# A streaming encoder layer on one core: another place for the last conv norms, and cross attention opened inside the last mixing tile

## The chip, the cores and the metric

One core of one Trainium2 chip runs the whole kernel in one launch. The metric is the device time of an execution in microseconds; the time of a kernel is the median of its runs.

## The reference

One layer of a chunk-causal hybrid encoder, in float32, for a prompt of 2048 frames and a sample group of 8 streams with 16 frames each (128 rows in all, which make a 17th tile beside the prompt's 16). D_MODEL is 1024.

```python
proj = h @ w_in                                   # h = rmsnorm(x, g_mix_pre)
q, k, v, u_val, u_gate = split(proj)              # 512 columns each
att = band_attention(q, k_ext, v_ext, ..., rel_bias)   # 8 heads x 64, own chunk of 64 + 8 previous
u = u_val * sigmoid(u_gate)
c = depthwise_conv(u_ext, conv_w) + conv_b        # causal, width 31, 512 channels
c = silu(layernorm(c, cln_g, cln_b))
y = concat([att, c]) @ w_out
x = x + rmsnorm(y, g_mix_post)
x = x + rmsnorm(memory_attention(rmsnorm(x, g_mem_pre), mk, mv, w_mq, w_mo), g_mem_post)
f = (silu(h @ w_gate) * (h @ w_up)) @ w_down      # h = rmsnorm(x, g_ffn_pre), hidden 2816
x = x + rmsnorm(f, g_ffn_post)
```

Memory attention has 4 heads of 256 and 256 memory tokens. For the prompt, its keys and values are made from `mem_prompt`; for the sample streams they are cached. The outputs are both groups' rows and the updated caches (attention K and V, conv rows, memory K and V).

## The kernel before

**Arithmetic.** Each float32 operand of a product is split into a high part (a rounded copy, made by a cast on ACT) and a low part (the difference, made by a subtraction on VectorE or on POOL). A product is three matmuls, high by high, high by low, low by high: `mm3` (L281 to L285, widths 128 to 384) and `mm3h` (L287 to L291, two halves of 512 columns, so six matmuls a block and 48 a tile).

**Stages.** `phase_mem` makes the memory's keys and values, and folds w_mq into the keys and w_mo into the values, so that cross attention has two weight blocks a row of blocks: f1 (scores) and f2 (values), eight blocks each. `phase_proj` makes q, k, v and the conv branch; `attention` runs the band attention; `mixout` applies w_out, tile by tile; `phase_cross`, `gate_up` and `down` follow.

**Projection.** Three groups of six tiles (the last has the sample tile in it), each in two sub-groups x = 0 and 1 of 384 and, in the last group, 256 prompt or sample columns. In a group come the GLU columns, then v, then K and Q by blocks j = 0 to 3. The depthwise convolution is a list of generators, `vq` for VectorE (L517 to L524) and `pq` for ACT and POOL (L526 to L533), pumped between the products at a rate per group and at low priority. `conv_norm` (L535 to L558) is the layer norm of one tile: four transposes to PSUM (L538), statistics on VectorE (L540, L542), the reciprocal root (L294 to L301), the normalised rows (L546), four transposes back (L550), scale and bias on ACT (L553), tanh (L556), the product (L557) and the store to the DRAM tensor `cs` (L558). Its result `z` has two buffers. Before the change the norms of the last group's first five tiles are put on `vq` in pairs behind the convolutions, ahead of the v products (`pairs(tiles[:-1], cts)`), and the sample tile's norm comes last. The scheduler of the framework then lists each engine's instructions; an engine runs its list in order.

**Q, K and the head load.** Each Q/K product is cast (L691, L697), its low part taken (L692, L698), and stored to DRAM (`qs`, `ks`, L717). `head_load` brings a head's q and k (L780, 64 rows of 2048) and v (L781) back; head 0's load is issued inside the last group. Tags of odd and even heads are apart, so two heads fit at a time.

**Attention.** 128 units of one head and one prompt tile: scores (L856), softmax on VectorE (L793) with the exponential on ACT (L795), transposes (L873), values (L886). Sample steps are mixed in (`sample`, L798 on); their bias rows `bs` are eight small DMAs (L899), and their scores L816.

**Mixing.** 17 tiles, sample first (L979 on). `prep` loads a tile's `cs` and splits it; then 48 products and the post norm (L1053 squares on ACT, L1057 on VectorE, L1058 on POOL, store of x1). Beside it the sample rows' cross attention runs as a filler (`cross_sample`, L1065 on), with L1086 as the load of its weight blocks (w_mq, cached keys and values, w_mo) and `postnorm` (L335 to L340, the residual on POOL at L340) at its end.

**Cross attention.** `phase_cross` opened after the last mixing tile: the gains (L362), norm(0) (x1 load L1218, `rms` L304 to L309, L315, transposes L318, high part L319 on ACT, low part L320 on VectorE), then all eight f1 blocks (load L1209 to one of three staging buffers `stg`, cast L1212 on ACT, subtraction L1213, on POOL for blocks 1, 3 and 5), norm(1), scores(0), and so on: scores (L1224 on), `probs` (L1242 on, transposes L1245, L1248, L1249), `values` (L1252 on). f2 blocks were loaded by `more`, behind the last exponential of scores(0) and the split of the first probabilities. `issue_after(x)` makes what is issued inside it stand behind x on its engine.

## Time and profile before

| | |
|---|---|
| runs | 2968.06, 2971.57, 2972.08 us; median 2971.57 |
| profiled execution | 2970.86 us, span 2969.1 us, mean granted clock 0.989 |
| TensorE, VectorE, ACT, POOL busy | 2877.8, 2076.6, 1308.7, 1367.9 us |
| DMA | 500.04 MB in 198474 packets, mean 168 GB/s |
| idle of TensorE, 600 to 680 us | 24.0 us |
| idle of TensorE, 1140 to 1180 us | 11.35 us |

A line of a timeline reads: start (us), duration, engine, source line, operation, output<-input, shape, count, and in brackets how long the engine had been idle and what ended that. The names of tiles are those of the memory pools (`psb` PSUM; `sbf`, `sbr`, `sbx`, `flexb` SBUF; `qs`, `ks`, `vs`, `cs`, `f1s` DRAM).

### The profile page before, as it was taken

What the parts mean: (1) busy time and instruction counts of PE and PEld (TensorE: products, weight loads), DVE (VectorE), ACT (ScalarE), POOL (GpSimd) and SP (SyncE); (2) the same over time, 40 slices, a digit from 0 to 9 for tenths busy, and PEclk for the clock granted to TensorE, in tenths of its full rate; (3) what the DMA queues carried; (4) which work ended last, traced back from release to release, by engine and by line L of the source; (5) the groups of instructions that cost most, each with busy time, mean ns of one, the idle gap of its engine ahead of it and who ended that gap; (6) DMA issues with size and microseconds to landing.
All of it is one profiled execution on the core that took longest, in us unless ns stands there. A gap on an engine that the chain in (4) does not pass through costs nothing.

```text
span 2969.1 us, 45382 instructions
## 1 busy us (share of the span) xinstructions
PE 2877.8 (97%) x16740; PEld 2628.1 (89%) x16740; DVE 2076.6 (70%) x3024; ACT 1308.7 (44%) x2661; POOL 1367.9 (46%) x1247
## 2 busy tenths in 40 slices
PE   8999999979989998999999999999999999999998
PEld 8999999968978776888879999999999999888786
DVE  6697795958985334445459888787888998546655
ACT  4535354648973223333334333433344444433433
POOL 0268395720022223145447656365656775424413
PEclk9999999989999999999999999999999999999999
DMA  8635255557845664223355333644434446756654
GB/s 307 245 114 179 91 167 161 169 154 188 214 144 175 229 219 164 76 96 126 112 172 196 138 114 133 200 155 152 145 121 160 148 143 211 242 172 221 226 193 165
DMA packets 198474, 500.04 MB, mean 168 GB/s; under 512 B 18981, under 2 KB 87085, under 8 KB 189923
## 3 DMA queue, kind: packets, MB, share of 16 engines
q1 hardware_dynamic: 187931, 461.09, 48.2%
q0 software_dynamic: 10320, 36.05, 3.1%
q8 instruction: 131, 2.15, 0.3%
q14 instruction: 92, 0.75, 0.1%
HBM read 365.97 MB, written 141.81 MB: 171 GB/s over the span
## 4 chain that ended last, share of the span: by engine, by line
PE 42%; DMA 3%; POOL 2%; DVE 2%; issue 1%; ACT 0%; DVEq 0%; SPq 0%; POOLq 0%; ACTq 0%
PE psb L285 13%; PE psb L284 13%; PE psb L283 13%; PE psb L291 1%; DMA sbf<-in_w_down_dram 1%; DMA sbf<-x 1%; POOL sbf L1500 1%; PE psb L1355 1%; DMA sbf<-hn 1%; POOL sbf L340 0%; DVE sbr L1378 0%; DMA hn<-sbf 0%; DVE flexb L1440 0%; DVE sbr L1561 0%; DVE sbx L1378 0%
## 5 line engine op out<-in xcount | busy, mean ns | idle before, releaser
L283 PE MATMUL psb<-sbr 128*128 128x384 f32 (+3 forms) x2808 | 942.1, 337 | 3.3 <-ACT sbr L319 1.1
L284 PE MATMUL psb<-sbr 128*128 128x384 f32 (+3 forms) x2356 | 805.6, 342 | 2.4 <-DVE sbr L320 2.4
L285 PE MATMUL psb<-sbr 128*128 128x512 f32 (+3 forms) x1848 | 632.7, 344 | 2.2 <-DVE sbr L1561 2.2
L283 PEld LDWEIGHTS psb<-sbr 128*128 128x128 f32 x2808 | 530.5, 189 | 32.5 <-ACT sbr L1357 1.7
L285 PE MATMUL psb<-sbr,sbx 128*128 128x384 f32 (+2 forms) x1484 | 476.8, 322 | 0.0
L284 PEld LDWEIGHTS psb<-sbr 128*128 128x128 f32 x2356 | 445.0, 189 | 29.4 <-DVE sbr L320 2.7
L285 PEld LDWEIGHTS psb<-sbr 128*128 128x128 f32 x1848 | 348.0, 189 | 30.6 <-DVE sbr L1561 4.2
L291 PE MATMUL psb<-sbr 128*128 128x512 f32 x1226 | 304.6, 397 | 12.5 <-ACT sbr L319 8.5
L1378 DVE TENSOR_TENSOR sbr<-sbf,sbr 128x512 fp32r<-128x512 f32 x258 | 263.3, 1023 | 38.0 <-ACT sbr L1377 37.2
L291 PEld LDWEIGHTS psb<-sbr 128*128 128x128 f32 x1226 | 227.8, 189 | 64.1 <-ACT sbr L319 9.0
L1377 ACT CAST sbr<-sbf 128x512 fp32r<-128x512 f32 x258 | 159.3, 620 | 277.3 <-PE psb L284 235.7
L285 PEld LDWEIGHTS psb<-sbr,sbx 128*128 128x128 f32 x1484 | 280.6, 189 | 0.2
L523 DVE SCALAR_TENSOR_TENSOR psb<-sbf,psb 128x768 f32<-128x768 f32 (+1 forms) x290 | 264.3, 912 | 6.2
L1561 DVE TENSOR_TENSOR sbr<-sbf,sbr 128x384 fp32r<-128x384 f32 (+1 forms) x231 | 163.0, 728 | 96.6 <-ACT sbr L1560 95.3
L278 POOL TENSOR_TENSOR sbx<-sbf,sbr 128x1024 fp32r<-128x1024 f32 x60 | 152.1, 2537 | 78.3 <-ACT sbr L277 73.7
L1560 ACT CAST sbr<-sbf 128x384 fp32r<-128x384 f32 (+1 forms) x231 | 111.0, 497 | 167.6 <-PE psb L284 146.2
L1500 POOL TENSOR_TENSOR sbf<-sbf 128x512 f32<-128x512 f32 x77 | 107.3, 1399 | 166.6 <-DMA sbf<-in_w_down_dram 165.1
L533 POOL TENSOR_TENSOR flexb<-flexb,flexb 128x128 f32<-128x128 f32 (+1 forms) x180 | 167.2, 929 | 21.3 <-ACT flexb L532 11.7
L283 PE MATMUL psb<-sbr,sbx 128*128 128x384 f32 (+1 forms) x524 | 170.5, 327 | 0.7 <-ACT sbr L1357 0.7
L1377 ACT CAST sbx<-sbf 128x512 fp32r<-128x512 f32 x153 | 94.7, 620 | 160.5 <-PE psb L284 151.1
L1378 DVE TENSOR_TENSOR sbx<-sbf,sbx 128x512 fp32r<-128x512 f32 x153 | 151.8, 994 | 15.0 <-ACT sbx L1377 14.6
L1372 POOL TENSOR_TENSOR sbf<-sbf 128x512 f32<-128x512 f32 x66 | 97.4, 1476 | 109.5 <-DVE sbr L1378 51.3
(322 smaller groups left out, 5910.4 us busy)
## 6 DMA issues: line engine op xcount, KB each, us to landing
af<-flexb SPq DMA_DIRECT2D x33, 1344.0 KB, 6.2
sbf<-in_w_down_dram SPq DMA_DIRECT2D x154, 256.0 KB, 3.7
sbf<-af SPq DMA_DIRECT2D x90, 384.0 KB, 4.0
sbf<-in_w_gate_dram SPq DMA_DIRECT2D x66, 512.0 KB, 3.3
sbf<-in_w_up_dram SPq DMA_DIRECT2D x66, 512.0 KB, 3.3
sbf<-x SPq DMA_DIRECT2D x49, 512.0 KB, 3.9
sbf<-in_w_in_dram SPq DMA_DIRECT2D x48, 512.0 KB, 3.9
sbr<-ks SPq DMA_DIRECT2D x28, 512.0 KB, 10.1
```

What stands on the lines that cost most here:

```text
L278: self.lo_engine.tensor_tensor(lo[:, :], wf[:, :], hi[:, :].bitcast(F32), ALU.subtract)
L283: nc.tensor.matmul(ps, lh, rh, start=start, stop=False, **kw)
L284: nc.tensor.matmul(ps, lh, rl, start=False, stop=False, **kw)
L285: nc.tensor.matmul(ps, ll, rh, start=False, stop=stop, **kw)
L291: nc.tensor.matmul(y[o], l, r[:, o * 512:(o + 1) * 512], start=start and x == 0, stop=stop and x == 2)
L523: nc.vector.scalar_tensor_tensor(acc if w < CW - 1 else o, src(w), cwt[:, j, w:w + 1], acc, ALU.mult, ALU.add)
L533: nc.gpsimd.tensor_tensor(o, o, v, ALU.add)
L1377: nc.scalar.copy(hs[j][:, :], src[j])
L1378: nc.vector.tensor_tensor(ls[j][:, :], src[j], hs[j][:, :].bitcast(F32), ALU.subtract)
L1500: nc.gpsimd.tensor_tensor(acc[:, :], acc[:, :], q[:, :], ALU.add if s > 0 else ALU.subtract)
L1560: nc.scalar.copy(ch[:, m], a[:, x, m])
L1561: nc.vector.tensor_tensor(cl[:, m], a[:, x, m], ch[:, m].bitcast(F32), ALU.subtract)
```

## The change

Instruction counts of all engines stay as they were. Lines behind L628 move (before, after): L691 is L688, L697 is L694, L707 is L704, L717 is L714, L780 and L781 are L789 and L790, L793 is L802, L856 is L865, L899 is L908, L1053 is L1070, L1086 is L1103, L1209, L1212 and L1213 are L1217, L1220 and L1221, L1245 is L1279.

First, the norms of the last group are not queued any more. The convolutions are emptied, then the four last Q/K products run, and behind each of them a fixed set of norm steps follows (`behind`), the sample's tile among them. These norms have a PSUM tag of their own, `nt`. The steps are issued behind the last product by name, but each engine's list is the scheduler's.

Second, the cross stage's buffers, its first gain, f1[0], f1[1] and norm(0) are made in `cross_open`, which is called inside the last mixing tile at k = 6, when the sample filler is exhausted; the twelve products left of that tile stand behind norm(0)'s transposes. The other f1 blocks and the first F2 blocks of f2 load behind the last w_mo load, as buffers come free. scores(0) follows whole, with norm(1) made inside it at k = 3; probs(0) is made inside scores(1) at k = 5. gpost loads after scores(0). The spots of f1, f2, stg, sh and sl in SBUF differ.

The core of the diff:

```diff
-            if last:
-                vq += pairs(tiles[:-1], cts)
...
             blks = {w: self.wload(A["w_in"][w * 4 + 3]) for w in (1, 0)}
+            if last:
+                while vq or pq:
+                    pump(vq or pq, 1)
+                norms = [conv_norm(t, cts, i * P, "nt") for i, t in enumerate(tiles)]
+            def behind(*steps):
+                with self.tc.issue_after(self.last_product.ins):
+                    for i, n in steps:
+                        for _ in range(n):
+                            next(norms[i], None)
             for x in range(2):
                 for w in (1, 0):
                     qk(w, 3, blks[w], x)
+                    if last:
+                        behind(*[((0, 1), (1, 1)), ((0, 2), (1, 2), (2, 1), (3, 1)),
+                                 ((2, 2), (3, 2), (4, 1)), ((4, 2),)][2 * x + 1 - w])
...
-            if last:
-                vq += pairs(tiles[-1:], cts, len(tiles) - 1)
...
+                if i == len(order) - 1 and k == 6:
+                    for _ in fill:
+                        pass
+                    self.cross_open()
+                    after = self.tc.issue_after(self.last_transpose.ins)
+                else:
+                    after = ExitStack()
+                with after:
+                    self.mm3h(y, mh[:, k, :], ml[:, k, :], ws[k][0], ws[k][1], k == 0, k == KC - 1)
...
+        with self.tc.issue_after(self.last_mo.ins):
+            f1 = [f1_load(k) for k in range(2)]
+            gpre = self.gain(pool, "g_mem_pre", "gpre")
+            hq = {0: norm(0)}
...
-        hq = {0: norm(0)}
-        f1 = [load(self.f1s[:, k, :, :].rearrange("p h n -> p (h n)"), f"f1{k}",
-                   nc.gpsimd if k in (1, 3, 5) else nc.vector) for k in range(KC)]
-        hq[1] = norm(1)
-        z = scores(*hq[0][1:], "y")
...
+        with self.tc.issue_after(self.last_mo.ins):
+            f1 += [f1_load(k) for k in range(2, KC)]
+            f2 = [load(self.f2s[:, k, :], f"f2{k}") for k in range(F2)]
+        with self.tc.issue_after(self.last_half.ins):
+            z = scores(*hq[0][1:], mid=(3, second))
+        gpost = self.gain(pool, "g_mem_post", "gpost")
+        first = self.last_half
+        with self.tc.issue_after(self.last_exp.ins):
+            f2 += [load(self.f2s[:, k, :], f"f2{k}") for k in range(F2, KC)]
```

How the lists move. TensorE at the end of projection, before (L283 to L285 are products, L538 and L550 the norms' transposes, L707 transposes of the output keys; 128x256 is sub-group x = 1, 128x384 x = 0):

```order
L283 MATMUL psb<-sbr 128x256
L284 MATMUL psb<-sbr 128x256
L285 MATMUL psb<-sbr,sbx 128x256
L538 MATMUL psb<-ident_73,flexb_157 128x128 x2
L550 MATMUL psb<-ident_73,flexb_153 128x128 x8
L538 MATMUL psb<-ident_73,flexb_157 128x128 x8
L550 MATMUL psb<-ident_73,flexb_153 128x128 x4
L707 MATMUL psb<-ident_73,sbf 128x128 x3
L283 MATMUL psb<-sbr 128x384
L284 MATMUL psb<-sbr 128x384
```

Twenty-two norm transposes stand here, and four more (L550) stand among the 384-wide products that follow. The same place after (L865 are the first attention scores, L704 the output keys' transposes):

```order
L283 MATMUL psb<-sbr 128x256
L284 MATMUL psb<-sbr 128x256
L285 MATMUL psb<-sbr,sbx 128x256
L865 MATMUL psb<-sbr 128x256 x4
L865 MATMUL psb<-sbr 128x128 x2
L550 MATMUL psb<-ident_73,flexb_153 128x128 x4
L538 MATMUL psb<-ident_73,flexb_157 128x128 x4
L550 MATMUL psb<-ident_73,flexb_153 128x128 x4
L538 MATMUL psb<-ident_73,flexb_157 128x128 x4
L865 MATMUL psb<-sbr 128x512 x2
```

Most of the norms' transposes now stand behind the last product, among the first scores.

SP's list after, from the load of head 1 on (`qs_10_82`, `ks_14_86` and `vs_18_90` are the DRAM copies of the first head pair's q, k and v, `cs_32` the norm of tile 12; the row ahead of these is the load of `qs_10_82`, twice, and the one ahead of that 512 KB of cached keys, L809):

```order
L789 DMA sbr<-ks_14_86 64x2048
L713 DMA out_dram<-sbf 128x512 x2
L714 DMA qs_13_85<-sbf 128x2x384
L789 DMA sbr<-ks_14_86 64x2048 x2
L713 DMA out_dram<-sbf 128x512
L714 DMA ks_17_89<-sbf 128x2x128
L789 DMA sbr<-ks_14_86 64x2048
L790 DMA sbr<-vs_18_90 128x2048
L811 DMA flexb_157<-in_cache_att_v_dram 128x2x512
L713 DMA out_dram<-sbf 128x512
L714 DMA qs_13_85<-sbf 128x2x128
L558 DMA cs_32_104<-flexb_153 128x512
```

Before, the norms' stores stood ahead of that load:

```order
L717 DMA qs_12_84<-sbf 128x2x128
L800 DMA sbf<-in_cache_att_kt_dram 128x4x256
L558 DMA cs_32_104<-flexb_153 128x512
L558 DMA cs_33_105<-flexb_153 128x512
L558 DMA cs_34_106<-flexb_153 128x512
L781 DMA sbr<-vs_18_90 128x2048
L717 DMA ks_17_89<-sbf 128x2x384
L558 DMA cs_35_107<-flexb_153 128x512
L780 DMA sbr<-qs_10_82 64x2048
L780 DMA sbr<-ks_14_86 64x2048 x2
```

The stores of tiles 12 to 14 moved from the front of head 1's load to behind it; those of tiles 13 to 16 follow there, and then the eight bias rows (L908).

ACT at the cross opening before (L1212 are casts of f1, L308 squares of a norm, L1053 squares of a mixing tile, L319 the first cross norm's high part):

```order
L308 ACTIVATE flexb_153<-psb 128x1024
L1212 CAST sbr<-sbf 128x1024
L1053 ACTIVATE flexb_153<-psb 128x512 x2
L1212 CAST sbr<-sbf 128x1024
L308 ACTIVATE sbf<-sbf 128x1024
L1212 CAST sbr<-sbf 128x1024 x2
L1053 ACTIVATE flexb_153<-psb 128x512 x2
L1212 CAST sbr<-sbf 128x1024
L319 CAST sbr<-psb 128x1024
```

Five f1 casts stand ahead of L319. After (L1220 are the casts, L1070 the squares):

```order
L1220 CAST sbr<-sbf 128x1024
L308 ACTIVATE sbf<-sbf 128x1024 x2
L1220 CAST sbr<-sbf 128x1024
L308 ACTIVATE flexb_153<-psb 128x1024
L1070 ACTIVATE flexb_153<-psb 128x512 x2
L1220 CAST sbr<-sbf 128x1024
L308 ACTIVATE sbf<-sbf 128x1024
L1220 CAST sbr<-sbf 128x1024 x3
L319 CAST sbx<-psb 128x1024
L1220 CAST sbr<-sbf 128x1024
L1070 ACTIVATE flexb_153<-psb 128x512 x2
```

Six casts stand ahead of L319 now, and the last mixing tile's squares moved from ahead of it to behind it.

More of the change, by code (lines that the diff above doesn't have):

```diff
@@ L284, in mm3 @@
         nc.tensor.matmul(ps, lh, rl, start=False, stop=False, **kw)
-        nc.tensor.matmul(ps, ll, rh, start=False, stop=stop, **kw)
+        self.last_product = nc.tensor.matmul(ps, ll, rh, start=False, stop=stop, **kw)
     def mm3h(self, y, lh, ll, rh, rl, start, stop):
@@ L290, in mm3h @@
             for o in range(2):
-                nc.tensor.matmul(y[o], l, r[:, o * 512:(o + 1) * 512], start=start and x == 0,
-                                 stop=stop and x == 2)
+                self.last_half = nc.tensor.matmul(y[o], l, r[:, o * 512:(o + 1) * 512], start=start and x == 0,
+                                                  stop=stop and x == 2)
     def rstd(self, pool, ss, scale):
@@ L317, in prenorm @@
         for k in range(KC):
-            nc.tensor.transpose(ps[:, k, :], h[:, k * P:(k + 1) * P], self.ident[:, :])
+            self.last_transpose = nc.tensor.transpose(ps[:, k, :], h[:, k * P:(k + 1) * P], self.ident[:, :])
         nc.scalar.copy(hi, ps[:, :, :])
@@ L533, in conv_pool, with conv_norm @@
                 nc.gpsimd.tensor_tensor(o, o, v, ALU.add)
-        def conv_norm(t, cts, off):
-            pt = self.t(ps_tr, [P, 4, P], F32, "tr")
+        def conv_norm(t, cts, off, tag="tr"):
+            pt = self.t(ps_tr, [P, 4, P], F32, tag)
             for j in range(4):
@@ L1067, in cross_sample @@
         gpre = self.gain(pool, "g_mem_pre", "sgain")
-        xt = self.t(pool, [P, D], F32, "xt", 2)
+        xt = self.t(pool, [P, D], F32, "kv")
         nc.sync.dma_start(xt[:, :], self.x1[S_TILE])
@@ L1085, in load @@
             wf = self.t(pool, [P, D], F32, "wf")
-            nc.sync.dma_start(wf[:, :], src)
+            self.last_mo = nc.sync.dma_start(wf[:, :], src)
             return wf
@@ L1222, in norm, with f1_load, phase_cross, scores @@
             return xt, hh, hl
-        def scores(hh, hl, where="s"):
+        def f1_load(k):
+            return load(self.f1s[:, k, :, :].rearrange("p h n -> p (h n)"), f"f1{k}",
+                        nc.gpsimd if k in (1, 3, 5) else nc.vector)
+        with self.tc.issue_after(self.last_mo.ins):
+            f1 = [f1_load(k) for k in range(2)]
+            gpre = self.gain(pool, "g_mem_pre", "gpre")
+            hq = {0: norm(0)}
+        self.cross = pool, ps_t, load, norm, f1_load, hq, f1
+    def phase_cross(self, ctx):
+        nc, A = self.nc, self.A
+        sbF, sbR = self.sbF, self.sbR
+        fr = Joined(*self.flex(ctx, *[(1024, F32R)] * 11))
+        pool, ps_t, load, norm, f1_load, hq, f1 = self.cross
+        ps_s = ps_y = ps_t
+        spots = ([(sbR, o) for o in (32, 36, 96, 100, 104)] +
+                 [(fr, 4 * i) for i in (7, 8, 9, 10, 6, 4, 3, 2, 5, 1, 0)])
+        for i, (arena, o) in enumerate(spots):
+            pool.at(f"f2{i // 2}{'hl'[i % 2]}", 4, (arena, [o]))
+        self.lo_engine = nc.vector
+        def scores(hh, hl, where="s", mid=None):
             s = self.t(ps_s, [P, 2, 512], F32, where)
             for k in range(KC):
+                if mid and k == mid[0]:
+                    mid[1]()
                 self.mm3h(halves(s), hh[:, k, :], hl[:, k, :], f1[k][0], f1[k][1], k == 0, k == KC - 1)
@@ L1229, in scores @@
             nmx = self.t(pool, [P, MH], F32, "nmx", 2)
-            nc.vector.tensor_reduce(nmx[:, :], sv, axis=AX.X, op=ALU.max, negate=True)
+            top = nc.vector.tensor_reduce(nmx[:, :], sv, axis=AX.X, op=ALU.max, negate=True)
+            if mid:
+                self.tc.keep_in_program_order(top)
             z = self.t(pool, [P, MH, NM], F32, "z", 2)
@@ L1288, in phase_cross, with second, opening @@
         todo = [(g, p) for g in range(3) for p in range(3)]
-        hq = {0: norm(0)}
-        f1 = [load(self.f1s[:, k, :, :].rearrange("p h n -> p (h n)"), f"f1{k}",
-                   nc.gpsimd if k in (1, 3, 5) else nc.vector) for k in range(KC)]
-        hq[1] = norm(1)
-        z = scores(*hq[0][1:], "y")
-        f2 = []
-        def more(n, event):
-            with self.tc.issue_after(event.ins):
-                for k in range(len(f2), min(len(f2) + n, KC)):
-                    f2.append(load(self.f2s[:, k, :], f"f2{k}"))
-        more(F2, self.last_exp)
+        def second():
+            hq[1] = norm(1)
+        def opening():
+            ready[0] = probs(z)
+        ready = {}
+        with self.tc.issue_after(self.last_mo.ins):
[7 more added lines that the diff above has]
+            f2 += [load(self.f2s[:, k, :], f"f2{k}") for k in range(F2, KC)]
         for t in range(NPT):
-            pp = probs(z) if t < NPT - 1 else self.last_probs
             if t == 0:
-                more(KC, self.last_split)
-            if t + 1 < NPT:
-                z = scores(*hq[t + 1][1:])
+                with self.tc.issue_after(first.ins):
+                    z = scores(*hq[1][1:], "y", (5, opening))
+                pp = ready.pop(0)
+            else:
+                pp = probs(z) if t < NPT - 1 else self.last_probs
+                if t + 1 < NPT:
+                    z = scores(*hq[t + 1][1:])
             if t + 2 < NPT:
```

25 lines of the change are left out of this document (8 added, 17 removed).

## The prediction

> **What bounds the kernel now.** I read the page first, then the busy time of each engine in stretches of 20 us, and then the two stretches in which TensorE is not full, on the timelines of each engine.
>
> ```profile
> span 2969.1 us, 45382 instructions
> PE 2877.8 (97%) x16740; PEld 2628.1 (89%) x16740; DVE 2076.6 (70%) x3024; ACT 1308.7 (44%) x2661; POOL 1367.9 (46%) x1247
> ```
>
> TensorE is busy for 97% of the span: the kernel ends when TensorE's list ends, and only its idle time (91 us in all) and time at a reduced clock can be won. The profiled execution took 2970.86 us, 0.7 below the median of 2971.57, so a sum against it is carried to the median unchanged. The stretches around the two places that the change touches come next. The columns are the window, its length, busy time (and count) of PE, PEld, DVE, ACT, POOL, then the granted clock, the DMA share and GB/s.
>
> ```profile
> 600.00:620.00 20.00, 16.55 (x125) 16.20 (x124) 17.15 (x28) 8.80 (x26) 10.32 (x24) 0.95 0.24 80
> 620.00:640.00 20.00, 15.94 (x75) 13.46 (x73) 6.62 (x12) 10.29 (x30) 2.26 (x4) 0.70 0.28 99
> 640.00:660.00 20.00, 11.41 (x58) 7.68 (x59) 10.13 (x30) 10.50 (x36) 1.77 (x7) 0.83 1.05 273
> 660.00:680.00 20.00, 12.10 (x85) 9.81 (x83) 9.78 (x24) 10.07 (x24) 0.99 (x1) 0.83 0.51 123
> ...
> 1120.00:1140.00 20.00, 20.00 (x91) 16.31 (x90) 6.64 (x7) 7.78 (x17) 7.88 (x11) 1.00 0.49 184
> 1140.00:1160.00 20.00, 8.71 (x40) 6.62 (x38) 9.62 (x8) 8.64 (x14) 15.19 (x15) 0.77 0.45 131
> 1160.00:1180.00 20.00, 19.94 (x81) 15.74 (x82) 8.36 (x8) 4.47 (x6) 5.36 (x3) 0.89 0.63 211
> ```
>
> Where projection turns into attention (600 to 680) TensorE is busy 56.0 of 80 us: 24.0 are idle. Where mixing turns into cross attention (1140 to 1180) it is busy 28.65 of 40: 11.35 are idle. In both places the granted clock is low as well. These two are what the change can reach; the other 56 us of idle time lie elsewhere.
>
> The waits of TensorE between 600 and 760, by releaser (total, count, longest), name the first place:
>
> ```profile
> PE psb L856 <- DVE flexb L793: 8.9, 5, 4.8
> PE psb L550 <- DVE flexb L546: 5.2, 2, 3.5
> PE psb L856 <- ACT flexb L695: 3.8, 1, 3.8
> ```
>
> The transposes of the conv norms (L538, L550) stand ahead of Q/K products that need nothing from them, and wait for VectorE's steps inside the norm.
>
> **Part A, the norm order.** The last Q/K products no longer stand behind norms. How much sooner does the first attention score come?
>
> ```profile
> 619.07 1.97 PE L550 MATMUL psb<-ident,flexb 128*128 128x128 f32 x8 [3.45 <-DVE flexb L546]
> ...
> 626.05 1.12 PE L550 MATMUL psb<-ident,flexb 128*128 128x128 f32 x4 [1.76 <-DVE flexb L546]
> ...
> 641.14 0.72 PE L856 MATMUL psb<-sbr 128*128 128x256 f32 x4
> ```
>
> The first score started at 641.14. Up to there TensorE idled 40 − 16.55 − 15.94 = 7.5 us (from 600). The order has 26 norm transposes between the K/Q products that end the projection; at 0.25 us (1.97 for 8) that is 6.5 us which now come later. The other 9.4 busy us of 620 to 640 ran at a clock of 0.70; at the full one they take 6.6, 2.8 less. Sum 16.8: the projection ends at about 624.3, without a stall, if its products find their operands (w_in blocks, loaded earlier) and a free accumulator (two casts of ACT and DVE, both idle half of the time there).
>
> But nothing is won yet: the norms still have to be done, and they are now the last thing ahead of the sample units. VectorE has the last convolution step behind it at 615.13, so it isn't the conv that they wait for. What they wait for is the stores of their results:
>
> ```profile
> 614.38 0.75 DVE L523 SCALAR_TENSOR_TENSOR flexb<-sbf,psb 128x512 f32<-128x512 f32 x1
> ```
> ```profile
> 624.45 6.38 SPq L558 DMA_DIRECT2D cs<-flexb  x3
> ...
> 655.83 12.45 SPq L899 DMA_DIRECT2D flexb<-toep  x8
> ```
> ```profile
> cs<-flexb SPq DMA_DIRECT2D x5, 256.0 KB, 2.9
> ```
>
> Before, the stores of tiles 12 to 14 were issued from 624.45 on, in an empty ring, and landed in 2.9 us (the median of five). In the new order they stand on SP behind the whole load of head 1: two q and four k blocks of 512 KB, 1 MB of v, 512 KB of cached v, four output rows of 256 KB, and three q/k stores of 128 to 384 KB; 6.1 MiB, with the cached k next to them 6.6 (6.4 to 6.9 MB). z has two buffers, so the ACT pass of norm 14 (L553) waits until the store of norm 12 has landed, and that of norm 16 for norm 14's. Everything that ACT has behind L553 waits too, the softmax exponentials of head 0 among it, and TensorE with them.
>
> ```profile
> q1 hardware_dynamic: 3524, 8.28, 84.7%
> sbr<-ks SPq DMA_DIRECT2D x4, 512.0 KB, 12.0
> ```
>
> The queue is served in order: with it full, the k loads took 12.0 us (632 to 670). It moved 8.28 MB in those 38 us, 0.218 MB/us, and 0.273 in the window that was full. So the 6.6 MB take 24 to 30 us; I take 27. They start at about 618 (the first of them follows the k store of the first half): norm 12's store lands at about 645. Then follow the steps of norm 14 and its store:
>
> ```profile
> 649.07 1.50 ACT L553 ACTIVATE flexb<-psb,sbf 128x128 f32<-128x128 f32 x4 [0.26 <-PE psb L550]
> ...
> 654.46 0.62 ACT L556 ACTIVATE flexb<-flexb 128x512 f32<-128x512 f32 x1
> ```
> ```profile
> 655.11 0.69 DVE L557 SCALAR_TENSOR_TENSOR flexb<-flexb 128x512 f32<-128x512 f32 x1 [0.23 <-ACT flexb L556]
> ...
> 669.88 0.44 DVE L793 CUSTOM_DVE_ANT_0 flexb<-psb,flexb 128x272 f32<-128x272 f32 x1 [5.22 <-DMA flexb<-toep]
> ```
>
> 1.50 + 0.62 + 0.69 + 2.9 = 5.7: norm 14's store lands at 651, norm 16 is stored at 654, the eight small bias rows (L899) follow it on SP and, the ring being empty by then, land at about 660. The first sample softmax, at 669.88 before, runs at 660: 10 us sooner. By VectorE's order two prompt softmaxes fewer stand ahead of it (16 instead of 18), and those are still owed:
>
> ```profile
> L793 DVE CUSTOM_DVE_ANT_0 flexb<-psb,flexb x107: 281/815/826, 699.8 to 877.4; 128x640 f32<-128x640 f32 x77, 128x128 f32<-128x128 f32 x6, 128x256 f32<-128x256 f32 x6, 128x384 f32<-128x384 f32 x6
> ```
>
> 177.6 us for 107 softmaxes, 1.7 us each, 3.4 for two. A is worth 10 − 3.4, about **6 us**, of the 16.8 that the projection's end gives. Bounds: if the stores weren't held at all, all 16.8 (taken as 16); if the ring moves at 0.218 from 622 on, norm 12 lands at 652, 7 later, a loss of 1, with a late row or two 3. I take 6, since the full ring's rows are those of this very load.
>
> A rule of the Trainium skill bears on the wait this leaves. In the trace the clock was 0.70 in 620 to 640, after gaps of up to 3.45 us, and 1.00 from 680 on. The Trainium skill, page TensorE: Matmul & The Clock Gate, section Part 1, has the clock halve after an idle window of about 3.4 us and return after as long a busy one. By that rule the wait in front of norm 16 would cost an estimated 1.7 us more and A would come to 4; the sum above leaves it out.
>
> **Part C, the cross opening.**
>
> ```profile
> 1146.33 1.03 PE L318 MATMUL psb<-ident,sbf 128*128 128x128 f32 x8
> 1155.83 1.22 PE L291 MATMUL psb<-sbr 128*128 128x512 f32 x2 [8.46 <-ACT sbr L319]
> ...
> 1159.87 1.22 PE L291 MATMUL psb<-sbr 128*128 128x512 f32 x2 [2.83 <-DVE sbr L1213]
> ```
> ```profile
> 1138.30 1.04 ACT L1212 CAST sbr<-sbf 128x1024 fp32r<-128x1024 f32 x1
> ...
> 1146.09 1.05 ACT L1212 CAST sbr<-sbf 128x1024 fp32r<-128x1024 f32 x1 [3.61 <-DMA sbf<-f1s]
> 1151.72 1.04 ACT L1212 CAST sbr<-sbf 128x1024 fp32r<-128x1024 f32 x1 [4.57 <-DMA sbf<-f1s]
> 1154.75 1.02 ACT L319 CAST sbr<-psb 128x1024 fp32r<-128x1024 f32 x1
> ```
>
> The transposes of the first cross norm were done at 1147.4, yet ACT copied them out (L319) only at 1154.75, since two casts of f1 stood ahead of it that waited for their loads: 8.46 us. The next wait, 2.83, is for a subtraction (L1213). Two matmuls took 1.22 us behind each, 0.61 apiece; the same product in the full stretch takes 0.227:
>
> ```profile
> L291 PE MATMUL psb<-sbr,sbx x23: 389/389/393, 1125.9 to 1130.9; 128*128 128x512 f32 x23
> ```
>
> So what is lost is 11.35 idle, 2.2 by the clock of 0.89 in 1160 to 1180, and about 1 before: 14.5 us.
>
> Now the transposes stand 12 products ahead of mixing's end: 1146.3 − 12 × 0.2275 = 1143.6. They find their input ready:
>
> ```profile
> 1137.17 1.29 DVE L315 SCALAR_TENSOR_TENSOR sbf<-sbf 128x1024 f32<-128x1024 f32 x1 [9.39 <-POOL sbf L301]
> ...
> 1141.28 1.22 DVE L1213 TENSOR_TENSOR sbr<-sbf,sbr 128x1024 fp32r<-128x1024 f32 x1
> ...
> 1156.45 3.37 DVE L1213 TENSOR_TENSOR sbr<-sbf,sbr 128x1024 fp32r<-128x1024 f32 x1
> ```
> ```profile
> 1145.11 2.38 POOL L1213 TENSOR_TENSOR sbr<-sbf,sbr 128x1024 fp32r<-128x1024 f32 x1
> ...
> 1155.42 3.31 POOL L1058 TENSOR_TENSOR flexb<-flexb 128x1024 f32<-128x1024 f32 x1 [0.31 <-DVE flexb L1057]
> ```
>
> L315 ended at 1138.5, 5 us ahead; the insertion costs TensorE nothing, and mixing ends at 1147.4. ACT has six f1 casts ahead of L319 now (five before). The first two loads come sooner, behind the last w_mo block; the others are bound by the three staging buffers. f1[4] can load when the POOL subtraction of f1[1] is done, about 1141.7 (cast at 1138.3, then 1.04 and 2.38):
>
> ```profile
> DMA to landing us min/median/max: 4.2/5.3/10.5
> ```
>
> By the smallest landing time of an f1 load its cast runs at about 1146, f1[5]'s by 1147.5, and L319 ends near 1149.5: TensorE waits some 2 us. The low part (L320) follows by 1.2 us, with four products of 0.9 us to cover it: 0.5 more, or 2.5 if VectorE's f1[4] subtraction takes 3.37 us beside a POOL pass instead of 1.22. Behind that the f1 blocks are there in time: a block feeds 1.37 us of products, and the load of f1[6] can start at 1146.5 for use near 1159. Left: 2.5 of the 14.5. C is worth **12 us** (bounds 8, with the long subtraction and median landings, and 14). The probabilities of the first tile and norm(1) only change places; gpost's later load has until the first value product's norm, 25 us on.
>
> The Trainium skill, page SBUF — State Buffer, section Who interferes with whom, says that a VectorE pass with two SBUF inputs and a GpSimd pass that reads SBUF lock each other out for the whole instruction. The trace agrees: 3.37 beside POOL's 3.31, else 1.22. By that rule C would be an estimated 2 us less whenever POOL's residual add lies beside f1[4].
>
> The rest (instruction counts, gate, up and down) is as it was. Sum: −6 − 12 = −18; 2970.86 gives 2952.9, the median of 2971.57 about **2953.5**.
>
> **Rivals.** *1, the ring eats A:* norm 12's store lands at 652 or later and A is worth between −2 and +3; C alone comes: about 2960. For it: a full ring at 0.218; against: 0.273 in the window that was full. *2, the stores aren't held:* they go out between the loads (the loads of head 1 wait for buffers, not SP); A gives 16: 2943. For it: 2.9 us for such stores before; against: SP's order. *3, the f1 loads bound C:* median landings of 5.3, a POOL pass beside each of three VectorE subtractions (2.15 apiece, 6.5 us); C gives 5: 2960. For it: the two waits of 3.61 and 4.57 for f1s; against: two blocks are in before mixing ends. *4, slower:* a head 1 load that stands ahead of norm 12's store on SP waits for its buffer until attention units of head 0 have run, which wait for ACT, which waits for that store's follower; every us that SP stands there is a us of TensorE. It decides from 18 us on (a landing at 663 instead of 645), and at 28 us gives 2981. For it: z's two buffers couple the two; against: odd and even heads have buffers of their own, and head 1 is the first odd one. *5:* the new order brings the same waits in other places, nothing changes.
>
> **How the numbers follow.** Chances: forecast 0.45, rival 1 0.22, 2 0.11, 3 0.11, 4 0.06, 5 0.05. What a measurement of this kernel can tell from no change is about 0.2%, 5.9 us, so faster means below 2965.6. The forecast, rival 2, most of rivals 1 (0.20) and 3 (0.10) are: 0.86; the same 0.08, with rival 5 and the remainder; slower 0.06. The range: low end A's 16 with C's 13 (2942.5, call it 2943); high end rival 1's loss of 3 with C's 8 (2966). It leaves out rivals 4 and 5 and the joint extremes.
>
> **What would show it.** In the changed profile: the first score near 624; ACT idle at L553 released by a cs store landing between 640 and 652, TensorE idle by 10 to 20 us in 625 to 650; the sample softmax near 660; full again by 680, about 6 us further in the list. At the opening, transposes L318 ahead of the last 12 products, a gap of 2 to 5 us instead of 8.46 and 2.83, L319 near 1148 (less A's gain), and no waits in the scores behind. I am wrong if the first score isn't earlier than 630, if cs lands within 4 us of its norm, or if the gap at the opening stays above 8 us.

## The result and the profile after

The changed kernel takes 2949.37 us (median of 4 runs, 2948.22 to 2957.10) beside 2971.43 us for the kernel before (4 runs, 2968.06 to 2972.08). The ratio is 0.9934, with a 95% interval of 0.9918 to 0.9949: faster by 15 to 24 us. Six later runs of the same kernel gave 2947.49 us and a ratio of 0.9923 (0.9910 to 0.9936). The profiled execution took 2949.61 us, 21.3 us below the 2970.86 of the one before. The head of its page:

```profile
span 2947.8 us, 45388 instructions
...
PE 2872.6 (97%) x16740; PEld 2624.6 (89%) x16740; DVE 2079.8 (71%) x3024; ACT 1308.1 (44%) x2661; POOL 1371.4 (47%) x1247
```

TensorE's instructions are as many as before; 16 us of the 21.3 came out of its idle time (91.3 before, 75.2 now: span less busy time) and 5 out of its busy time. The windows of the two stretches (columns as in the prediction: PE, PEld, DVE, ACT, POOL, granted clock, DMA share, GB/s):

```profile
600.00:620.00 20.00, 20.00 (x138) 19.90 (x138) 15.79 (x25) 12.03 (x42) 9.23 (x20) 1.00 0.33 109
620.00:640.00 20.00, 13.83 (x91) 11.10 (x89) 12.82 (x31) 9.63 (x30) 4.58 (x12) 0.83 1.01 273
640.00:660.00 20.00, 9.90 (x51) 7.68 (x52) 8.39 (x22) 11.39 (x28) 0.88 (x3) 0.57 0.56 192
660.00:680.00 20.00, 19.27 (x159) 16.81 (x157) 18.26 (x44) 18.46 (x47) 0.99 (x1) 1.00 0.50 116
...
1120.00:1140.00 20.00, 15.86 (x68) 12.37 (x67) 11.82 (x7) 13.20 (x24) 17.58 (x17) 0.88 0.57 186
1140.00:1160.00 20.00, 20.00 (x94) 16.63 (x93) 15.52 (x17) 8.56 (x15) 7.84 (x7) 0.95 0.57 197
```

Projection now runs full to 620 and beyond; the hole lies in 620 to 660; and from 660 on TensorE is full at the full clock, where before 660 to 680 was still 12.10 busy at 0.83. The hole at the cross opening shrank from 11.35 us to 4.14. The waits of TensorE in the two stretches, before them the first score, and the end of the longest wait:

```profile
624.53 0.82 PE L865 MATMUL psb<-sbr 128*128 128x256 f32 x6
...
645.22 1.12 PE L550 MATMUL psb<-ident,flexb 128*128 128x128 f32 x4 [8.23 <-ACT flexb L553]
```
```profile
PE psb L550 <- ACT flexb L553: 8.2, 1, 8.2
PE psb L882 <- ACT flexb L553: 3.6, 2, 3.1
...
PE psb L291 <- ACT sbx L319: 2.2, 1, 2.2
PE psb L291 <- DVE sbx L320: 2.0, 1, 2.0
```

What ACT waited for, and when the first sample softmax ran (timelines of ACT and VectorE, and SP's issue of the store of tile 12):

```profile
635.11 0.32 SPq L558 DMA_DIRECT2D cs<-flexb  x1
```
```profile
643.66 1.50 ACT L553 ACTIVATE flexb<-psb,sbf 128x128 f32<-128x128 f32 x4 [6.16 <-DMA cs<-flexb]
```
```profile
658.93 0.44 DVE L802 CUSTOM_DVE_ANT_0 flexb<-psb,flexb 128x272 f32<-128x272 f32 x1 [0.29 <-DMA flexb<-toep]
```

The store of norm 12 released ACT at 643.66, and the bias rows released the first sample softmax at 658.93, eleven us sooner than before.

**Where the time went, stage by stage.** TensorE has 16740 instructions in every version, so the start of its n-th one can be compared between kernels: at each point of the table the instructions ahead are the same by shape in every version, only in another order. The table gives start minus start in the kernel before, at the end of projection (n = 3800, 579.4 us before), the start of mixing (5810, 887.3), shortly ahead of the cross opening (7000, 1107.5) and behind it (7300, 1188.8), the start of down (15600, 2692.9), and the last instruction's end. A is the difference of the first two, C that of the next two. The first row is another execution of the kernel before: what it shows is what one execution can move without any change.

| kernel | 3800 | 5810 | 7000 | 7300 | 15600 | end | A | C |
|---|---|---|---|---|---|---|---|---|
| before, again | 0.0 | -1.0 | -1.3 | -3.8 | -3.1 | -0.9 | -1.0 | -2.5 |
| changed | -0.1 | -15.1 | -15.4 | -24.7 | -24.6 | -21.5 | -15.0 | -9.3 |
| changed, again | -1.9 | -17.9 | -18.3 | -27.1 | -25.3 | -26.0 | -16.0 | -8.8 |
| e1 norms alone | +0.8 | -13.3 | -12.9 | -13.7 | -16.7 | -14.0 | -14.1 | -0.8 |
| e2 cross alone | +0.8 | -0.5 | -0.9 | -11.4 | -10.9 | -7.7 | -1.3 | -10.5 |
| e3 stores by POOL | +1.1 | -12.0 | -12.0 | -22.0 | -20.7 | -18.6 | -13.1 | -10.0 |
| e4 casts behind L319 | +0.7 | -13.8 | -14.0 | -18.2 | -13.1 | -9.7 | -14.5 | -4.2 |
| e5 low part first | +5.2 | -10.5 | -11.2 | -20.1 | -22.2 | -22.2 | -15.7 | -8.9 |
| e6 five buffers | +0.8 | -13.3 | -13.7 | -23.8 | -24.3 | -22.5 | -14.1 | -10.1 |
| e7 head 1 later | -1.9 | -16.1 | -16.0 | -25.9 | -24.4 | -20.9 | -14.2 | -9.9 |
| e8 buffers and bias rows | -1.2 | -26.1 | -26.9 | -37.5 | -35.5 | -32.3 | -24.9 | -10.6 |
| e9 bias rows alone | -0.5 | -13.9 | -14.2 | -23.4 | -25.0 | -23.5 | -13.4 | -9.2 |
| e12 five buffers, clear | +0.3 | -15.2 | -15.4 | -26.7 | -27.3 | -26.2 | -15.5 | -11.3 |

### The profile page after: what moved, and what is told of

Read it like the earlier page. It is cut to its first block, busy times and chain, and to the rows that moved or that the text cites. A ratio compares the mean times of both kernels' runs of the same rounds, so it can differ in the third digit from the quotient of the medians.

```text
span 2947.8 us, 45388 instructions
## 1 busy us (share of the span) xinstructions
PE 2872.6 (97%) x16740; PEld 2624.6 (89%) x16740; DVE 2079.8 (71%) x3024; ACT 1308.1 (44%) x2661; POOL 1371.4 (47%) x1247
## 3 DMA queue, kind: packets, MB, share of 16 engines
q8 instruction: 131, 2.15, 0.3%
## 4 chain that ended last, share of the span: by engine, by line
PE 43%; DMA 3%; POOL 2%; DVE 2%; issue 1%; ACT 0%; DVEq 0%; SPq 0%; POOLq 0%; ACTq 0%
PE psb L285 14%; PE psb L284 14%; PE psb L283 14%; PE psb L291 1%; DMA sbf<-in_w_down_dram 1%; DMA sbf<-x 1%; POOL sbf L1540 1%; PE psb L1395 1%; DMA sbf<-hn 1%; DVE sbr L1601 0%; POOL sbf L340 0%; DMA hn<-sbf 0%; DMA sbf<-in_w_gate_dram 0%; DVE flexb L1480 0%; DVE sbr L1418 0%
## 5 line engine op out<-in xcount | busy, mean ns | idle before, releaser
L283 PE MATMUL psb<-sbr 128*128 128x384 f32 (+3 forms) x2808 | 943.0, 337 | 3.7 <-ACT sbr L1600 1.5
L285 PE MATMUL psb<-sbr 128*128 128x512 f32 (+3 forms) x1848 | 633.9, 345 | 1.9 <-DVE sbr L1601 1.8
L283 PEld LDWEIGHTS psb<-sbr 128*128 128x128 f32 x2808 | 530.6, 189 | 33.6 <-ACT sbr L1600 2.6
L285 PE MATMUL psb<-sbr,sbx 128*128 128x384 f32 (+2 forms) x1484 | 476.7, 322 | 0.0
L284 PEld LDWEIGHTS psb<-sbr 128*128 128x128 f32 x2356 | 445.3, 189 | 29.5 <-DVE sbr L320 2.7
L285 PEld LDWEIGHTS psb<-sbr 128*128 128x128 f32 x1848 | 348.5, 189 | 31.4 <-DVE sbr L1601 4.6
L285 PEld LDWEIGHTS psb<-sbr,sbx 128*128 128x128 f32 x1484 | 280.5, 189 | 0.2
L291 PE MATMUL psb<-sbr 128*128 128x512 f32 x1004 | 247.3, 395 | 0.1
L291 PEld LDWEIGHTS psb<-sbr 128*128 128x128 f32 x1004 | 185.8, 188 | 41.5 <-issue 2.5
L1540 POOL TENSOR_TENSOR sbf<-sbf 128x512 f32<-128x512 f32 x77 | 106.2, 1385 | 169.2 <-DMA sbf<-in_w_down_dram 167.6
L533 POOL TENSOR_TENSOR flexb<-flexb,flexb 128x128 f32<-128x128 f32 (+1 forms) x180 | 167.4, 931 | 22.4 <-ACT flexb L532 12.9
L283 PE MATMUL psb<-sbr,sbx 128*128 128x384 f32 (+1 forms) x524 | 170.5, 327 | 1.2 <-ACT sbr L1397 0.7
L291 PE MATMUL psb<-sbr,sbx 128*128 128x512 f32 x654 | 160.7, 397 | 4.1 <-ACT sbx L319 2.2
```

The costliest lines, as they stand in the source:

```text
L283: nc.tensor.matmul(ps, lh, rh, start=start, stop=False, **kw)
L284: nc.tensor.matmul(ps, lh, rl, start=False, stop=False, **kw)
L285: self.last_product = nc.tensor.matmul(ps, ll, rh, start=False, stop=stop, **kw)
L291: self.last_half = nc.tensor.matmul(y[o], l, r[:, o * 512:(o + 1) * 512], start=start and x == 0, stop=stop and x == 2)
L533: nc.gpsimd.tensor_tensor(o, o, v, ALU.add)
L1540: nc.gpsimd.tensor_tensor(acc[:, :], acc[:, :], q[:, :], ALU.add if s > 0 else ALU.subtract)
```

## The experiments

All run on one core with the kernel before beside them; times are medians, ratios are against the kernel before, with their 95% intervals.

**e1 and e2, the two parts apart.** e1 has the hunks of the projection only, e2 those of mixing and cross attention only. The core of each, against the kernel before:

```diff
 e1
-                vq += pairs(tiles[:-1], cts)
+                norms = [conv_norm(t, cts, i * P, "nt") for i, t in enumerate(tiles)]
+                        behind(*[((0, 1), (1, 1)), ((0, 2), (1, 2), (2, 1), (3, 1)),
+                                 ((2, 2), (3, 2), (4, 1)), ((4, 2),)][2 * x + 1 - w])
 e2
+                if i == len(order) - 1 and k == 6:
+                    self.cross_open()
```

> The norm order alone; the cross stage opens as before. Theory: the norm order is worth 15 us by itself (half of it idle time of TensorE, half a higher clock), so the mixing starts about 15 us sooner than before and the time is about 2956. Rival: 6 us of it are its own, as predicted, and the rest needs the other part: about 2965.

> The cross opening alone; the norms stand as before. Theory: 9 us, so about 2962, with two waits of about 2 us each left at the opening. Rival: the predicted 12 us come where the first part's lead doesn't shift the loads: about 2959. If the 3 us that were given back at the end (down) belong to this part, 2965.

Measured: e1 2957.33 us, ratio 0.9956 (0.9942 to 0.9971); e2 2962.06 us, 0.9969 (0.9957 to 0.9981). The two savings add up to 0.75% of the time; both parts together give 0.66% and 0.77% in the two sets of runs. In the table e1 has A alone (14.1) and e2 C alone (10.5). So the norm order is worth about 14 us by itself and 15 to 16 beside the other part, not 6. The opening came to 9 to 10.5 in these profiles, below the 12 of the prediction, but by a margin that one execution can move: the kernel before, unchanged, has -2.5 in that column, and the interval of e2's ratio reaches from 5.6 to 12.8 us.

**e3, another queue for the stores.**

```diff
-            nc.sync.dma_start(self.cs[t], z[:, :, :].rearrange("p a b -> p (a b)"))
+            (nc.gpsimd if tag == "nt" else nc.sync).dma_start(self.cs[t], z[:, :, :].rearrange("p a b -> p (a b)"))
```

> The changed kernel, with the six last norm stores issued on POOL's queue instead of SP's. Theory: the stores behind head 1's load are what ACT and TensorE wait for (8.2 and 3.1 us): the stores land some 3 us after their issue, the first sample softmax comes at about 651 instead of 658.9, and the time is 5 to 9 us below the changed kernel's, 2941 to 2944. Rival: the bias rows and the cached values still come behind the full ring, so that the wait only moves to them: 0 to 3 us, 2946 to 2949.

Measured: 2949.38 us, 0.9925 (0.9909 to 0.9941): no gain over the changed kernel. Five stores moved, not six: the last group is tiles 12 to 15 and the sample's, 16 (and so four of its norms, not five, stood ahead of the v products before the change). POOL issued the store of norm 12, and ACT went on (timelines of POOL and ACT):

```profile
633.32 0.69 POOL L558 DMA_DIRECT2D cs<-flexb  x1 [2.59 <-DVE flexb L557]
```
```profile
642.22 2.98 ACT L553 ACTIVATE flexb<-psb,sbf 128x128 f32<-128x128 f32 x8 [4.61 <-DMA cs<-flexb]
651.33 1.50 ACT L553 ACTIVATE flexb<-psb,sbf 128x128 f32<-128x128 f32 x4 [3.97 <-DMA cs<-flexb]
```

On a queue of its own, with nothing ahead of it there, the store still took 8.9 us from 633.32 to 642.22; from SP it took 8.5. POOL's queue isn't slow by itself: eleven other stores of 256 KB from it (`hn`) landed in 3.2 us, the median in this trace. So my theory on record falls in its form: what holds the store is for the most part not its place in SP's list (that is worth 3 us: in the changed kernel the result was ready at 632.2 and the store issued at 635.11), but the traffic that the DMA engines are busy with (their share was 1.01 of full in 620 to 640 of the changed kernel, the row above).

**e6 and e12, five buffers for the norms' results.** That is one for each norm of the last group. e6 has the fifth buffer in another place; e12 the ones shown.

```diff
+                   .at("zn", 2, (fa, [4, 6]), (sbF, [20, 32.5, 8]))
-            z = self.t(pool, [P, 4, P], F32, "z", 2)
+            z = self.t(pool, [P, 4, P], F32, "z" if tag == "tr" else "zn")
```

> The changed kernel, with five buffers for the norms' results instead of two. Theory: with the stores on POOL's queue the landings stayed at 642 to 644, so it is the traffic of head 1's load that holds them, whichever queue they are on, and ACT waits since the buffers are two. With five ACT doesn't wait at L553, TensorE's 8.2 and 3.1 us go, and the bias rows, which still stand behind the stores and the traffic, bind next at about 652 instead of 658.9: 4 to 8 us, 2941 to 2945. Rival: the bias rows bind at the same time as before, since SP and the traffic set them: 0 to 2 us, 2947 to 2949.

> The changed kernel, with the five buffers of the norms' results in the places that they have together with the early bias rows; the bias rows stay where they were. It takes away the overlap of the first trial of five buffers, in which a step of VectorE stood behind a norm store. Theory: the bias rows, which follow the norm stores on SP and share the traffic, bind as before: the first sample softmax at 654 to 657, the mixing start as in the changed kernel within 2 us, 2945 to 2949. Rival: that overlap was the whole wait, and five buffers alone give what both gave: 2939 to 2941.

Measured: e6 2945.39 us, 0.9907 (0.9892 to 0.9923); e12 2944.77 us, 0.9911 (0.9895 to 0.9927). ACT no longer waits at L553 in either. In e6 TensorE's wait moved to the softmax (7.1 us at the longest), and VectorE stood behind a small step, L953, whose place the fifth buffer overlapped:

```profile
654.83 0.15 DVE L953 TENSOR_TENSOR flexb<-ident 16x8 f32<-16x8 f32 x1 [7.53 <-DMA cs<-flexb]
...
656.51 0.44 DVE L802 CUSTOM_DVE_ANT_0 flexb<-psb,flexb 128x272 f32<-128x272 f32 x1 [0.48 <-DMA flexb<-toep]
```

With that out of the way, in e12, VectorE waits for the bias rows themselves (SP's list, then VectorE):

```profile
645.23 1.22 SPq L558 DMA_DIRECT2D cs<-sbf  x2
647.90 4.83 SPq L908 DMA_DIRECT2D flexb<-toep  x8
```
```profile
654.27 0.44 DVE L802 CUSTOM_DVE_ANT_0 flexb<-psb,flexb 128x272 f32<-128x272 f32 x1 [3.82 <-DMA flexb<-toep]
```

The rows stand on SP behind the last norm stores, then wait there for 1.4 us until the store of a norm has landed whose buffer their place overlaps, and their eight issues take 4.83 us.

A is 14.1 and 15.5 in their profiles, as in the changed kernel (15.0 and 16.0). The medians are 3 to 4 us below it, but the intervals of the ratios overlap, so a gain of their own is not shown. What is shown is that the wait for the stores had another one right behind it.

**e9 and e8, the bias rows.** e9 gives the eight bias rows a place that is free early; SP then issues them at 610, ahead of head 1's load. e8 is e9 and the buffers of e12 together.

```diff
-.lay(fa, 5, ("otmp", 2, 1), ("bs", 1.0625, 1))
+.lay(fa, 5, ("otmp", 2, 1)).at("bs", 1.0625, (sbF, [48.5]))
```

> The changed kernel, with the sample's bias rows in a place of their own and loaded early; the norms' results keep two buffers. Theory: the stores hold ACT as in the changed kernel (8.2 and 3.1 us), the bias rows weren't the last to arrive (VectorE waited 0.29 us for them): 0 to 2 us, 2947 to 2949. Rival: the bias rows were the bound by themselves: as much as with five buffers, 2941 to 2944.

> The changed kernel, with five buffers for the norms' results and the sample's bias rows in a place of their own, so that they load before the traffic of head 1. Theory: with five buffers alone the wait moved to the sample softmax behind the bias rows (7.1 us); with those out of the way, no wait of the norms is left, the first sample softmax comes near 645 instead of 658.9, and the mixing starts 5 to 8 us sooner than in the changed kernel: 2941 to 2944. Rival: the traffic of 8 MB binds again at another place (cached values, head 1's keys), as when head 1 was loaded late: 2948 to 2950.

Measured: e9 2949.47 us, 0.9927 (0.9914 to 0.9941), no gain; e8 2938.82 us, 0.9896 (0.9882 to 0.9911), below the changed kernel's 2947.49 and 0.9923 (0.9910 to 0.9936) of the same set, though the ends of the intervals touch (0.9911, 0.9910); in its profile A is 24.9. The sample softmax and the stretch in e8:

```profile
639.26 0.44 DVE L802 CUSTOM_DVE_ANT_0 flexb<-psb,sbf 128x272 f32<-128x272 f32 x1 [0.18 <-PE psb L825]
```
```profile
620.00:640.00 20.00, 16.21 (x97) 12.30 (x96) 13.66 (x37) 14.75 (x46) 4.87 (x15) 0.79 1.02 279
640.00:660.00 20.00, 18.27 (x137) 16.50 (x137) 16.65 (x41) 16.36 (x40) 1.53 (x1) 0.87 0.56 200
```

TensorE is busy for 18.27 of the 20 us in which the changed kernel had 9.90. Neither condition alone does it (A 15.5 and 13.4), both together do (24.9): two waits in parallel, for stores that hold ACT and for rows that hold VectorE. Head 1's traffic holds the stores; the rows stand behind the stores in SP's list and wait for the buffer of one of them. In time the gain shows as well: of the six later runs of the changed kernel one (2944.85) lies among the five of e8 (2935.89 to 2945.61), the others above. In e9 the first sample softmax ran early too, and it helped nothing:

```profile
649.05 0.43 DVE L802 CUSTOM_DVE_ANT_0 flexb<-psb,sbf 128x272 f32<-128x272 f32 x1
```

e12 also answers my prediction's rival 2 ("the stores aren't held"): with the stores harmless A stayed at 15, since it did not say what would be late next.

**e7, head 1 loaded later.**

```diff
+            self.last_cs = nc.sync.dma_start(self.cs[t], z[:, :, :].rearrange("p a b -> p (a b)"))
...
-                    self.head_load(h + 1, heads[h + 1], 0, NPT)
+                    with self.tc.issue_after(self.last_cs.ins) if h == 0 else ExitStack():
+                        self.head_load(h + 1, heads[h + 1], 0, NPT)
```

> The changed kernel, with the load of head 1 put behind the last norm store on SP. Theory: the stores land in some 3 us, no wait for them is left, and the first sample softmax comes near 645; head 1 is loaded by 665, and its first units wait for it by 0 to 5 us. 5 to 10 us: 2940 to 2944. Rival: the wait is only moved, TensorE stands as long at head 1's first score as it stood at the norms: 2948 to 2952.

Measured: 2950.12 us, 0.9927 (0.9915 to 0.9939): no gain, as the rival had it, but only in part for its reason. With head 1's load out of their way the five norm stores landed in 2.9 us (median; 8.5 in the changed kernel), which confirms that this traffic held them. But there are two buffers still: ACT waited 1.56 and 3.70 us at L553 for stores to land, and TensorE stood 2.7 and 6.2 us behind it. The sample softmax came at 651.93, and the lead over the kernel before was 19.5 us at TensorE's instruction 4300, against 12.8 in the changed kernel; at 4500 it was back at 13.6 (12.9). In between stands the wait for head 1's keys, and a stretch that is not full:

```profile
PE psb L882 <- ACT flexb L553: 6.2, 1, 6.2
PE psb L550 <- ACT flexb L553: 2.7, 1, 2.7
PE psb L865 <- DMA sbr<-ks: 2.0, 1, 2.0
PE psb L865 <- DVE flexb L802: 2.0, 3, 0.9
PE psb L834 <- POOL flexb L829: 1.9, 1, 1.9
```
```profile
660.00:680.00 20.00, 17.97 (x131) 16.40 (x130) 16.25 (x44) 16.33 (x41) 0.00 (x0) 1.00 1.02 246
680.00:700.00 20.00, 18.11 (x140) 16.97 (x139) 14.85 (x37) 15.21 (x36) 1.47 (x4) 0.91 0.95 239
```

The DMA share is full 40 us later than in the changed kernel: the traffic was moved, and a part of the wait with it.

**e4, f1 casts behind the first norm's high part.**

```diff
-            f1 += [f1_load(k) for k in range(2, KC)]
+            f1 += [f1_load(k) for k in range(2, 4)]
+            with self.tc.issue_after(self.last_hi.ins):
+                f1 += [f1_load(k) for k in range(4, KC)]
```

`last_hi` is the first norm's L319.

> The changed kernel, with the casts of f1 blocks 4 to 7 put behind the first cross norm's high part on ACT. Theory: the first wait at the opening (2.2 us) was for these casts and goes; with it go the slow clock behind it and most of the second wait, since the f1[4] subtraction is out of VectorE's way: 3 to 6 us, 2943 to 2946. Rival: the second norm's scaling beside POOL's residual add still holds the low part: the second wait grows by what the first loses, 0 to 1 us, 2948 to 2949.

Measured: 2953.96 us, 0.9935 (0.9916 to 0.9953): no gain, C down to 4.2 in the profile. That profile is of the slowest of four runs (2961.48 us, the others 2947.48 to 2956.64), so how much was lost is not shown; which waits came and went is. The waits for L319 and L320 are both gone, as the theory had it, and others stand in their place, further into the scores. TensorE's waits, and VectorE:

```profile
PE psb L291 <- DVE sbr L1221: 4.1, 2, 3.1
PE psb L291 <- ACT sbr L1282: 3.6, 1, 3.6
```
```profile
1143.38 1.41 DVE L1074 SCALAR_TENSOR_TENSOR flexb<-psb,flexb,sbf 128x512 f32<-128x512 f32 x2 [8.02 <-DMA x<-flexb]
1144.71 4.53 DVE L1221 TENSOR_TENSOR sbr<-sbf,sbr 128x1024 fp32r<-128x1024 f32 x2
```

Moving the casts changed VectorE's list as well: the subtractions of the last f1 blocks now stand behind the scaling of the last mixing tile (L1074), which waited 8.02 us for the store of the tile ahead to leave its buffer. This is a wait that neither theory named.

**e5, the low part first.**

```diff
-            hq[1] = norm(1)
+            with self.tc.issue_after(first_lo.ins):
+                hq[1] = norm(1)
...
+                    if k in (4,):
+                        c.enter_context(self.tc.issue_after(first_lo.ins))
```

`first_lo` is the first norm's L320.

> The changed kernel, with the second norm's scaling and f1[4]'s subtraction put behind the first norm's low part on VectorE; ACT's order and the subtractions of f1[5] to f1[7] stay. Theory: the second wait at the opening (2.0 us) was the low part standing behind the second norm's scaling, which took 3.38 us beside POOL's residual add; it goes, and the first wait (2.2 us, the casts) stays. 2 to 4 us below the changed kernel: about 2946. Rival: another wait takes its place, as when the casts were moved: no gain, 2949 or more.

Measured: 2951.95 us, 0.9932 (0.9920 to 0.9945): no gain, C 8.9. The first norm's low part follows its high part at once and TensorE doesn't wait for it; the second norm's low part now comes late, behind the third norm's scaling, which took 3.40 us beside a POOL add of 3.45:

```profile
1137.17 1.23 DVE L320 TENSOR_TENSOR sbx<-psb,sbx 128x1024 fp32r<-128x1024 f32 x1 [4.96 <-ACT sbx L319]
...
1148.99 3.40 DVE L315 SCALAR_TENSOR_TENSOR sbf<-sbf 128x1024 f32<-128x1024 f32 x1
1152.32 1.21 DVE L1221 TENSOR_TENSOR sbx<-sbf,sbx 128x1024 fp32r<-128x1024 f32 x1
1153.45 1.21 DVE L320 TENSOR_TENSOR sbr<-psb,sbr 128x1024 fp32r<-128x1024 f32 x1
```
```profile
1154.72 9.40 PE L291 MATMUL psb<-sbr 128*128 128x512 f32 x33 [2.63 <-DVE sbr L320]
```

**e10 and e11, both kernels once more.**

> The kernel before once more, unchanged. Theory: one execution differs from another by up to 3 us ahead of the projection's end and in the last stage (down), which the change doesn't touch; so the 3 us that the changed kernel's profile loses in down against that of before are of the execution. Rival: down takes the same time in both executions of before, and the loss is the change's.

> The changed kernel once more, unchanged, to set its time and its stages beside these runs: about 2949, the mixing 15 us and the values 24 us sooner than before.

Measured: e10 2970.09 us (one run), e11 as told above. In e10 the stages lie up to 5.7 us ahead of the first execution (at the start of gate and up) and lose 4.8 of that by the end. The loss in down that the changed kernel's first profile shows (24.6 at its start, 21.5 at its end) is not the change's: the same kernel in e11 gained 0.7 there (25.3 to 26.0), and the unchanged one in e10 lost 2.2 (3.1 to 0.9). Of the two profiles of the kernel before, the first was the quicker one in down.

## Why the prediction was right, and where a term was mis-sized

The forecast was 2953.5 us (range 2943 to 2966); measured were 2949.37 and 2947.49. Its sum was -6 for A and -12 for C. Measured in the profile: -0.1 ahead of A, -15.0 for A, -0.3 between the two, -9.3 for C, and +3.2 behind them, together -21.5 at TensorE's last instruction. Point by point:

- *Projection ends at 624.3.* The first score started at 624.53. Right, and by the three terms: from 600 to the first score TensorE idled 0.1 us (8.2 before), 8 norm transposes stood ahead of it (29 before), and the clock was full.
- *Norm 12's store lands at 645, and ACT's L553 waits for it.* It released ACT at 643.66 after 6.16 us; TensorE's longest wait was 8.23. Right in time, wrong in part in the cause: I put it down to SP's order, which held the store for 3 us. Then it took 8.5 us to land, where a quiet stretch needs 2.9: that is the traffic, and e3 shows that it holds a store of POOL's queue as well.
- *The first sample softmax at 660.* 658.93.
- *"A is worth 10 - 3.4".* This is the step that failed. I read the gain off one event and took off two softmaxes as owed. It was one: nine softmaxes stood ahead of the sample's before and eight after, each with a row that reads its sum (18 and 16 rows). And the lead at one event isn't the lead of TensorE, whose list goes on in another order there: in e9 the event came 20.8 us sooner than before, and A was 13.4. Before, from the first sample softmax at 669.88 on, TensorE still had the rows that the prediction quotes: 12.10 busy in 660 to 680 at a clock of 0.83. After, it was full at 1.00 from 660 on. The term has to be taken over the whole stretch in which the two differ, busy time included. From 600 to the start of mixing, with the same instructions, first before and then after:

```profile
600.00:887.30 287.30, 254.87 (x1873) 226.53 (x1871) 231.53 (x540) 221.13 (x547) 40.94 (x69) 0.94 0.68 176
```
```profile
600.00:872.20 272.20, 247.06 (x1872) 221.93 (x1871) 231.67 (x540) 220.92 (x548) 41.32 (x69) 0.95 0.71 185
```

  15.1 us shorter: 7.3 of them idle time (32.4 and 25.1), 7.8 busy time (254.9 and 247.1). Half of the gain of A was in no wait at all, but in matmuls that ran quicker. Most of that is the clock: by the clock records of the two traces, TensorE was busy at half the clock for 21.5 us of the first stretch and 11.2 of the second, worth some 5 us (an estimate, half the difference). The prediction counted the clock up to the first score, and not behind it.
- *C: "Left: 2.5 of the 14.5".* Left were 4.1 us of waits, and slow matmuls behind them. The first, L319, was as worked out (2.2 against 2): the casts of f1[4] and f1[5] stood ahead of it and waited 1.66 and 1.57 us for their loads. The second, L320, was put at 0.5, or 2.5 if a subtraction of f1[4] fell beside a POOL pass. It was 2.0, from another instruction of the same kind:

```profile
1132.95 3.38 DVE L315 SCALAR_TENSOR_TENSOR sbf<-sbf 128x1024 f32<-128x1024 f32 x1
1136.25 1.21 DVE L320 TENSOR_TENSOR sbx<-psb,sbx 128x1024 fp32r<-128x1024 f32 x1
```
```profile
1131.90 3.34 POOL L340 TENSOR_TENSOR flexb<-flexb,sbf 128x1024 f32<-128x1024 f32 x1
```
```profile
1134.21 1.34 PE L291 MATMUL psb<-sbr,sbx 128*128 128x512 f32 x4 [2.18 <-ACT sbx L319]
1137.52 5.51 PE L291 MATMUL psb<-sbr,sbx 128*128 128x512 f32 x14 [1.96 <-DVE sbx L320]
```

  norm(1)'s scaling took 3.38 us beside POOL's residual add, else 1.29, and the low part stood behind it. And the fourteen products after it took 5.51 us, 0.39 each where the full stretch has 0.227: 2.3 us that the sum had not charged, since it took the clock for full behind short waits. The Trainium skill, page TensorE: Matmul & The Clock Gate, section Part 1, has the clock halve after an idle window of about 3.4 us. The traces agree on the length, and not on the idleness: the granted clock changes only at steps of 3.41 us, but a step needn't be idle to cost it. Here the clock halved at 1135.10, between the two waits, at the end of a step in which TensorE had been busy for 1.23 us, and was full again at 1141.92. Nor was the wait of 8.23 us (637.0 to 645.2) what took the clock in 640 to 660: it was at half from 633.34 on, ahead of that wait. The length of a wait doesn't decide either: in e12 one of 2.09 us at the opening cost the clock, and the fourteen products took 4.92 us; in e8 one of 2.69 us fell across two steps, with 2.15 and 1.87 us of work, the clock stayed full, and they took 3.48. The measurement decides; the last section has the count. (The 0.61 apiece that the prediction set beside 0.227 is a poor measure of the clock: a row of two such products shows 0.61 us at the full clock too, 0.305 apiece, as at 1112.26 in the kernel before.)
- *Rivals.* 1 (the ring eats A) and 5 (no change) didn't come: A was 13 or more in every execution with the norm order. 2 was near in time (16 for A) but not in mechanism: the stores were held, and letting them go alone (e12) changed A by nothing that shows. 3 (f1 loads) came in part, with waits of 1.66 and 1.57. 4, the slower side, needed norm 12 to be held to 663; it was released at 643.66.

The two errors, 9 too little in A and 3 too much in C, have opposite signs, and so the sum (18) lies nearer to the 19.6 of the ratio (0.66% of 2971.43) than its terms do to theirs. That is luck: with A alone right in size the forecast would have been 2944.5, 5 us too low.

The version to take is e8: 2938.82 us, 33.9 below the 2972.72 of the kernel before in the same set.

## What to carry to other kernels

When a stall is moved, price it over the whole stretch in which the two orders differ, idle and busy time of the bounding engine both; one event's lead says little, since slow matmuls behind gaps can weigh as much as the gaps. When a wait for a DMA is found, ask first whether its queue or the traffic holds it (another queue for the same transfer tells), and then what stands ready to be late next: here a wait for stores and a wait for rows behind them hid each other, and only removing both paid. A reordering by one engine's edges can change another engine's list; read all lists before the run.
